# Seven block products for the last branch's gates, and blocks in the output projection

## The chip, the cores and the metric

The kernel runs on one core of a Trainium2 chip. The metric is the device time of one execution in microseconds (us), the median of several runs on the chip. Engines: PE is TensorE (matmuls), DVE is VectorE, ACT is ScalarE, POOL is GpSimd, SP issues the transfers (DMA) between DRAM and the on-chip memory. Each engine works through its own queue of instructions in order and waits there for what an instruction needs.

## The reference

Two layers of: a SwiGLU feed-forward (half weight), a token mixer, a second feed-forward, each between two RMS norms and added to a residual `x` of 512 tokens x 1024. What the change touches is the end of the mixer:

```python
def rms_norm(x, g):
    xf = x.astype(jnp.float32)
    y = xf * lax.rsqrt(jnp.mean(xf * xf, axis=-1, keepdims=True) + NORM_EPS)
    return (y * g.astype(jnp.float32)).astype(x.dtype)
...
    proj = h @ w_in                        # h = rms_norm(x, norm_pre[l, 1])
    ...
    branches = jnp.stack([sb_out, conv_out, gla_out], axis=2)         # each (512, 512)
    branch_d = jnp.einsum('bsgw,gwd->bsgd', branches, w_branch)       # to 1024
    gates = jax.nn.sigmoid(gate_logits.reshape(b, s, N_BRANCHES, D_MODEL))
    merged = jnp.sum(gates * branch_d, axis=2)
    return merged @ w_out
...
        x = x + rms_norm(m, norm_post[l, 1])
```

`gate_logits` are the last 3 x 1024 columns of `proj`. The three branches are stick-breaking attention, a depthwise convolution with layer norm, and gated linear attention.

## The kernel before

**Numbers.** Each float32 factor is split into a rounded part and a rest (`split`, `whi` and `wlo` for weights, `xh` and `xl` for the normalised input). A product is three matmuls: high by high, high by low, low by high. A weight tile arrives by DMA in `raw`, ACT casts `whi` from it, DVE subtracts to get `wlo`.

**Layout.** The mixer's input lies transposed in `xh`, `xl`: 8 k tiles of 128 channels, 512 tokens. A gate (`gate_branch`) for 128 output channels `d` is 8 k tiles x 3 matmuls with 512 tokens moving, in the bank `gate`, a sigmoid on ACT (`gs`), then the branch product: 4 k tiles x 3 matmuls in the bank `pb`, and DVE multiplies `gs<-pb,gs`. POOL adds it to `acc[d]`. `gates(g, ...)` runs over eight `d`; branch 0 (attention) fills `acc`, branch 2 (linear attention) comes next, and branch 1 (convolution) is last, because the convolution's 124 taps run on DVE beside the first two. In the loop over `gla_gates`, after the sixth gate, the convolution's norm is finished (`y<-cb`, `brl<-y`, `branch_split`).

After each gate of the last branch, `merge(d)` splits `acc[d]` into `mh`, `ml`. `out_proj` with `head=None` then multiplies them by `w_out`: 8 k tiles x 4 token tiles x 2 halves x 3 matmuls, of which the last four k tiles (`TAIL`) are done token tile by token tile, so that one tile's norm, residual and next norm (`Hand`) run beside the next tile's matmuls.

**Blocks of the feed-forward.** The feed-forward stages already use Strassen-Winograd's seven products: `block_tiles` takes two column tiles of the weights (gate and up) and two halves of the tokens as a 2 x 2 block matrix. Each product is 4 k tiles x 3 matmuls with 256 tokens moving. DVE forms sums of raw weights (`raw<-raw`); the sums of inputs are the forms `T1` to `T4` of the class `Forms`, built as the tokens arrive. `AHEAD` says how many products ahead the weights are prepared. The class `Down` does the same for the down projection, 16 of its 22 k tiles in blocks with pairs `c` (`PER` of them), and the rest plainly. Its seven products are named A12, A11, S3, S2, A22, S1, S4.

**Order.** A scheduler of the framework sets each engine's order from the program; instructions in `pinned(...)`, and all matmuls, keep the order in which they are written. The residual lies in four tiles `x_sb[i]` for the whole kernel.

Of the kernel before, what the change touches and what calls it, by code (L numbers as in the profile page):

```python
# [13 lines left out]
P = 128  # L14
D = 1024
# [26 lines left out]
def kernel(  # L42
# [19 lines left out]
    sm = ctx.enter_context(tc.tile_pool(name="sm", bufs=4))  # L62
    psp = ctx.enter_context(tc.tile_pool(name="psp", bufs=1, space=PSUM))
# [237 lines left out]
    def out_proj(w2d, nk, stat, tail, finish, upcoming, early, head=None):  # L301


        ld = lambda k: load_rows(w2d, k)
        fresh = head is None
        if fresh:
            banks = [[bank(f"o{i}{h}", "pb" if i < 3 else "pa") for h in range(2)] for i in range(NT)]
        else:
            banks, rest = head

        def mms(i, h, k, sh, sl, wh, wl):
            mm_out(banks[i][h], slice(i * P, (i + 1) * P), sh, sl, wh[:, HS[h]], wl[:, HS[h]],
                   fresh and k == 0, k == nk - 1)
# [83 lines left out]
    class Forms:  # L397
# [26 lines left out]

        def finish(self, n):
# [23 lines left out]
    def block_tiles(w0, w1, fs, forms, hid, between):  # L449
# [4 lines left out]
        silu = lambda o, i: pin(nc.scalar.activation(o, i, AF.Silu))  # L454
# [3 lines left out]
        n = 7 * len(fs)  # L458
        raw, banks, cps, ring = {}, {}, {}, {}

        def load(u):
            r = wp.tile([P, 5, 512], F32, tag="raw", name="raw", bufs=3)
            for w, q0 in ((w0, 0), (w1, 1)):
                for j in range(2):
                    nc.sync.dma_start(r[:, q0 + 2 * j].rearrange("p (k c) -> p k c", c=P),
                                      w[j * 512:(j + 1) * 512, fs[u] * P:(fs[u] + 1) * P]
                                      .rearrange("(k p) c -> p k c", p=P))
            raw[u] = r
# [46 lines left out]
        def parts(u):  # L515
            cp = cps[u]
            return [cp[:, x * 256:(x + 1) * 256] for x in range(4)], hid[fs[u]], banks[u]

        def taken(g):
# [11 lines left out]
            if j == 6:  # L531
                silu(h[:, H0], h[:, H0])
                silu(h[:, H1], A[:, H0])

        def summed(g):
# [8 lines left out]
            if j == 6:  # L544
                tt(h, cps[u][:, 512:1024], h, ALU.mult)

        for g in range(-AHEAD, n + 1):
            between(g)
            f = g + AHEAD
            if f % 7 == 0 and f < n:  # L550
                if f == 0:
                    load(0)
                if f // 7 + 1 < len(fs):
# [15 lines left out]
    class Down:  # L569
        F0, NP = 2, 8  # L570
        R1, R2 = slice(256, 512), slice(0, 256)
        PER = NP // 2
# [4 lines left out]
        MIDDLE, LAST = (0, 1), (18, 19, 20, 21)  # L577

        def __init__(self, wd, hid):
            self.wd, self.hid = wd, hid  # L580
            self.ready = {}
            self.s1 = None
# [50 lines left out]

        def sums(self, p):
# [7 lines left out]
            kept = None if j < 2 else self.kept[:, 2 * c:2 * c + 2, :].rearrange("p k c -> p (k c)")  # L642
# [4 lines left out]
            if name == "S2":  # L647
                for q, x in enumerate(self.of(p)):
                    tt(x, self.s1[c][:, q], x, ALU.add)
                tt(kept, kept, raws[0], ALU.subtract)  # L650
# [52 lines left out]
        def run(self, late):  # L703
            c0, d0, c1, d1, b0, b1 = (bank(n) for n in ("oC", "oD", "oC", "oD", "oB", "oB"))
# [3 lines left out]
            self.kept, taps = room("xh", F32), room("xl", F32)  # L708
# [8 lines left out]
            for p in range(self.end):  # L717
                j, c = self.steps[p]
                self.product(p)
                self.ahead()  # L720
# [9 lines left out]
                if j == 5:  # L730
# [13 lines left out]
            return self.out, rest  # L744
# [32 lines left out]
    def ffn(wg, wu, wd, weights, forms, arrive, finish, upcoming, early, late, begin):  # L777
# [71 lines left out]
        down = Down(wd, hid)  # L849
        block_tiles(wg, wu, fs, forms, hid, between)  # L850
# [4 lines left out]
    def mixer(l, wv, arrive, finish, upcoming, early):  # L855
# [24 lines left out]

        cw = mp.tile([P, 4, NR], F32, tag="cw", name="cw")
# [295 lines left out]
        def gate_branch(g, d, src, wb):  # L1177
# [4 lines left out]
            wh, wl = wb  # L1182
# [5 lines left out]
            return pb, sg  # L1188
# [13 lines left out]
        def gates(g, src, done):  # L1202
            for d in range(0, KC, 2):
                wb = load_branch(g, d)
                for dd in (d, d + 1):
# [7 lines left out]
                    if done is not None:  # L1213
                        done(dd)
                    yield

        sb_gates = gates(0, branch_split(sbT, "s"), None)
# [82 lines left out]
        gla_gates = gates(2, branch_split(glaT, "t"), None)  # L1300
# [24 lines left out]

        for u_ in range(KC):
            next(gla_gates)
            conv_taps(10)
            if u_ == 3:
# [18 lines left out]
        merged = []  # L1348

        def merge(d):  # L1350
            tag = "t" if d < 4 else "q"
            mh, ml = slot("mh", F32R, tag), slot("ml", F32R, tag)
            split(mh, ml, acc[d])
            merged.append((mh, ml))
# [22 lines left out]
    for idx, (l, s) in enumerate(subs):  # L1377
        norms = []

        def late():  # L1380
            norms.append(load_g(norm_post[l, s]))
            if idx + 1 < len(subs):
                norms.append(load_g(norm_pre[subs[idx + 1][0], subs[idx + 1][1]]))

        if s == 1:
            late()
# [25 lines left out]
        elif s == 1:  # L1412
            weights = mixer(l, weights, arrive, finish, upcoming, early)
# [32 lines left out]
```

## Time and profile before

| | |
|---|---|
| median of 3 runs | 2326.82 us (2326.2 to 2327.48) |
| the profiled execution | 2326.21 us, span 2324.5 us |
| PE | 2301.7 us, 99% of the span |
| DVE | 1849.0 us, 80% |
| ACT | 1220.9 us, 53% |
| POOL | 165.0 us, 7% |
| granted clock of PE | 0.999 |
| moved by DMA | 265.29 MB, mean 114 GB/s |

The span is the time between the first and the last instruction of one execution. Busy times are sums over instructions that may overlap their neighbours, so the price of one of many in a row is the distance of their starts.

### The profile page before, as it was taken

How to read it: one execution, taken by the hardware profiler on the slowest of the kernel's cores; microseconds unless marked ns; L12 is line 12 of the kernel's file. 1: busy time of each engine (PE TensorE's matmuls, PEld its weight loads, DVE VectorE, ACT ScalarE, POOL GpSimd, SP SyncE). 2: the span in 40 equal slices, each digit the busy share in tenths (PEclk: the TensorE clock that was granted, in tenths of full speed). 3: DMA queues.
4: the chain of work that ended last, by engine and by line, in shares of the span. 5: the costliest groups of instructions: out<-in, count | busy, mean ns of one | idle time of the engine just before them, and what ended most of it. 6: DMA issues, size and time to landing. Idle time of an engine off the chain costs nothing.

```text
span 2324.5 us, 35435 instructions
## 1 busy us (share of the span) xinstructions
PE 2301.7 (99%) x13688; PEld 2035.6 (88%) x13688; DVE 1849.0 (80%) x2755; ACT 1220.9 (53%) x2370; POOL 165.0 (7%) x277
## 2 busy tenths in 40 slices
PE   8999999999999999999999999999999999999998
PEld 7999888887888889998889998888878888899987
DVE  7888987859965388889888889878599644888897
ACT  5565656644323355656555666566433333566664
POOL 0000001201021100000000000022010211000000
PEclk9999999999999999999999999999999999999999
DMA  5333644131333223336433336532313332333363
GB/s 174 100 101 110 227 153 119 55 105 47 109 91 109 82 73 100 100 110 232 149 87 98 107 112 233 155 105 63 93 55 109 91 91 81 91 99 103 115 221 109
DMA packets 333019, 265.29 MB, mean 114 GB/s; under 512 B 13003, under 2 KB 285421, under 8 KB 332849
## 3 DMA queue, kind: packets, MB, share of 16 engines
q1 hardware_dynamic: 332848, 263.02, 37.3%
q8 instruction: 107, 1.75, 0.3%
q14 instruction: 64, 0.52, 0.1%
HBM read 260.88 MB, written 2.10 MB: 113 GB/s over the span
## 4 chain that ended last, share of the span: by engine, by line
PE 97%; DVE 1%; ACT 1%; issue 0%; DMA 0%; SPq 0%; DVEq 0%; POOLq 0%; ACTq 0%
PE A L66 19%; PE gate L66 11%; PE C L66 9%; PE oA L66 9%; PE pb L66 6%; PE oC L66 5%; PE B L66 5%; PE o L66 3%; PE oB L66 3%; PE pf L66 3%; PE gr L66 2%; PE pa L66 2%; PE q L66 2%; PE gv L66 2%; PE pv L66 2%; PE pgl L66 2%
## 5 line engine op out<-in xcount | busy, mean ns | idle before, releaser
L455 DVE TENSOR_TENSOR wlo<-raw,whi 128x1024 fp32r<-128x1024 f32 (+1 forms) x304 | 331.0, 1089 | 107.0 <-ACT whi L453 106.1
L453 ACT CAST whi<-raw 128x512 fp32r<-128x512 f32 x532 | 315.2, 620 | 164.7 <-DVE raw L455 164.7
L115 ACT CAST whi<-raw 128x1024 fp32r<-128x1024 f32 (+2 forms) x178 | 185.0, 1045 | 351.9 <-PE gate L66 131.4
L116 DVE TENSOR_TENSOR wlo<-raw,whi 128x1024 fp32r<-128x1024 f32 (+2 forms) x178 | 223.0, 1262 | 174.0 <-ACT whi L115 169.3
L455 DVE TENSOR_TENSOR raw<-raw 128x512 f32<-128x512 f32 x304 | 209.2, 688 | 5.7
L66 PE MATMUL A<-xh,whi 128*128 128x256 f32 x608 | 172.5, 284 | 0.0
L66 PE MATMUL A<-xh,wlo 128*128 128x256 f32 x608 | 172.0, 283 | 0.0
L66 PE MATMUL A<-xl,whi 128*128 128x256 f32 x608 | 172.0, 283 | 0.0
L1031 DVE SCALAR_TENSOR_TENSOR y<-u,cw,y 128x511 f32<-128x511 f32 (+14 forms) x240 | 166.8, 756 | 0.0
L66 PE MATMUL gate<-xh,whi 128*128 128x512 f32 x384 | 151.3, 394 | 0.0
L66 PE MATMUL gate<-xh,wlo 128*128 128x512 f32 x384 | 149.8, 390 | 1.3 <-DVE wlo L116 1.3
L66 PE MATMUL gate<-xl,whi 128*128 128x512 f32 x384 | 149.6, 390 | 0.0
L674 DVE TENSOR_TENSOR wlo<-raw,whi 128x1024 fp32r<-128x1024 f32 x104 | 127.0, 1222 | 17.5 <-ACT whi L671 17.5
L671 ACT CAST whi<-raw 128x1024 fp32r<-128x1024 f32 x104 | 109.4, 1052 | 59.3 <-issue 17.0
L268 POOL TENSOR_TENSOR rs<-ms,mhalf 128x1 f32<-128x1 f32 x44 | 25.1, 575 | 1436.9 <-DVE ms L266 1436.9
L453 ACT COPY cp<-A 128x256 f32<-128x256 f32 x228 | 84.3, 370 | 66.6 <-PE A L66 65.7
L66 PE MATMUL oA<-wlo,dh 128*128 128x512 f32 x304 | 118.6, 390 | 0.0
L66 PE MATMUL oA<-whi,dl 128*128 128x512 f32 x304 | 118.3, 389 | 0.0
L66 PE MATMUL oA<-whi,dh 128*128 128x512 f32 x304 | 118.3, 389 | 0.0
L66 PEld LDWEIGHTS A<-xl,whi 128*128 128x128 f32 x608 | 116.6, 192 | 0.2
L66 PEld LDWEIGHTS A<-xh,whi 128*128 128x128 f32 x608 | 116.5, 192 | 0.2
L66 PEld LDWEIGHTS A<-xh,wlo 128*128 128x128 f32 x608 | 116.6, 192 | 0.0
(329 smaller groups left out, 6945.6 us busy)
## 6 DMA issues: line engine op xcount, KB each, us to landing
raw<-in_ffn_w_down_dram SPq DMA_DIRECT2D x152, 512.0 KB, 4.5
raw<-in_w_in_dram SPq DMA_DIRECT2D x108, 512.0 KB, 4.7
raw<-in_ffn_w_gate_dram SPq DMA_DIRECT2D x168, 256.0 KB, 3.4
raw<-in_ffn_w_up_dram SPq DMA_DIRECT2D x168, 256.0 KB, 4.5
raw<-in_w_branch_dram SPq DMA_DIRECT2D x24, 512.0 KB, 3.6
raw<-in_w_out_dram SPq DMA_DIRECT2D x16, 512.0 KB, 4.1
g<-in_norm_pre_dram SPq DMA_DIRECT2D x6, 512.0 KB
g<-in_norm_post_dram SPq DMA_DIRECT2D x6, 512.0 KB
```

The lines of the kernel that those rows point to most:

```text
L66: tc.keep_in_program_order(nc.tensor.matmul(*a, **k))
L115: pin(nc.scalar.copy(hi, src))
L116: pin(nc.vector.tensor_tensor(lo, src, hi.bitcast(F32), op=ALU.subtract))
L268: nc.gpsimd.tensor_tensor(self.rs, ms, mhalf[:, 0:1], op=ALU.pow)
L453: copy = lambda o, i: pin(nc.scalar.copy(o, i))
L455: tt = lambda o, a, b, op: pin(nc.vector.tensor_tensor(o, a, b, op=op))
L671: pinned(nc.scalar.copy(hi, src))
L674: pinned(nc.vector.tensor_tensor(lo, src, hi.bitcast(F32), op=ALU.subtract))
L1031: nc.vector.scalar_tensor_tensor(y[:, back:], u[:, :S - back], cw[:, c, j:j + 1], y[:, back:], op0=ALU.mult, op1=ALU.add)
```

## The change

1. The last branch's gates go through `block_tiles`: four pairs of column tiles, seven products each, with `AHEAD` of 4 products (6 in the feed-forward). The branch products of a pair stay plain matmuls and stand after the pair's seven products (`branch_products`).
2. The forms `T1` to `T4` are needed in the mixer too. They are not built when the tokens arrive, but from `xh` and `xl` in `Forms.rebuild`, called after the last two gates of branch 2. `T1` and `T2` are kept in the room of the residual tiles `x0` to `x3`. The residual is stored to DRAM (`away`) at the mixer's start and loaded again (`back`) in the middle of the output projection; the two norm weights that were loaded at the mixer's start are loaded there too.
3. The output projection runs k tiles 0 to 3 through `Down` with one pair (`PER` = 1), and 4 to 7 plainly. `merge` and its splits go. The sums `down.sum` at the hand-over of tokens come in, as in the feed-forward.

The core of the diff:

```diff
+        def rebuild(self, c, room_):
+            tt = lambda o, a, b, op: nc.vector.tensor_tensor(o, a, b, op=op)
+            def whole(k0, t0):
+                r = slot("r", tag="s").rearrange("p (k t) -> p k t", k=2)
+                at = (slice(None), slice(k0 + 2 * c, k0 + 2 * c + 2), slice(t0, t0 + 256))
+                tt(r, cur["xh"][at].bitcast(F32), cur["xl"][at].bitcast(F32), ALU.add)
+                return r
+            def keep(n, r):
+                hi, lo = room_(n)
+                split(hi, lo, r)
+                self.parts.setdefault(n, [None] * 4)[2 * c:2 * c + 2] = [(hi[:, k], lo[:, k]) for k in range(2)]
+            r11, r12 = whole(0, 0), whole(0, 256)
+            tt(r12, r11, r12, ALU.subtract)
+            keep("T1", r12)
+            r22 = whole(4, 256)
+            nc.vector.scalar_tensor_tensor(r22, r12, -1.0, r22, op0=ALU.mult, op1=ALU.subtract)
+            keep("T2", r22)
+            tt(r11, r22, r11, ALU.add)
+            keep("T3", r11)
+            r21 = whole(4, 0)
+            tt(r21, r22, r21, ALU.add)
+            keep("T4", r21)
...
-        def run(self, late):
+        def run(self, late, order=("C0", "D0", "C1", "D1", "B0", "B1")):
...
                 self.product(p)
-                self.ahead()
+                if self.PER > 1:
+                    self.ahead()
...
+                    if not self.MIDDLE:
+                        sh, sl, hi, lo = self.ready[self.end]
+                        for i in range(2):
+                            mm_out(self.out[i][1], slice(i * P, (i + 1) * P), sh, sl, hi[:, HS[1]], lo[:, HS[1]], st=True)
+                if self.PER == 1:
+                    self.ahead()
...
+        away = [scr.tile([P, D], F32, tag=f"away{i}", name=f"away{i}") for i in range(NT)]
+        for i in range(NT):
+            nc.sync.dma_start(away[i], x_sb[i])
...
         for u_ in range(KC):
             next(gla_gates)
             conv_taps(10)
+            if u_ >= KC - 2:
+                mforms.rebuild(u_ - KC + 2, form_room)
...
-        for _ in gates(1, cv, merge):
-            pass
-        return out_proj(w_out[l], KC, lambda k: merged[k], TAIL, finish, upcoming, early)
+        down = Down(w_out[l], acc, 0, 2, (), (4, 5, 6, 7))
+        down.pairs()
+        PAIRS = KC // 2
...
+        def sigmoids(u, h, a, second):
+            pinned(nc.scalar.activation(h[:, H0], h[:, H0], AF.Sigmoid))
+            pinned(nc.scalar.activation(h[:, H1], a, AF.Sigmoid))
+            pinned(nc.scalar.activation(second, second, AF.Sigmoid))
...
+        def merged(u):
+            if u > 0:
+                for d in (2 * u - 2, 2 * u - 1):
+                    for n in range(2):
+                        down.sum_tokens(d, n)
+            for m, (ps, sg) in enumerate(zip(pbs[u], made[u])):
+                pinned(nc.vector.tensor_tensor(sg, ps, sg, op=ALU.mult))
+                d = 2 * u + m
+                (nc.vector if u == PAIRS - 1 else nc.gpsimd).tensor_tensor(acc[d], acc[d], sg, op=ALU.add)
+
+        def between(g):
+            u, j = divmod(g, 7)
+            if 0 <= u < PAIRS and j == 2:
+                held[0] = True
+                wbs[u] = load_branch(1, 2 * u)
+                held[0] = False
+            if u > 0 and j == 0:
+                branch_products(u - 1)
+            if u > 0 and j == 1:
+                merged(u - 1)
+            if g in (7 * PAIRS - 2, 7 * PAIRS - 1, 7 * PAIRS):
+                down.ahead()
+
+        block_tiles(source, PAIRS, mforms, target, sigmoids, between, 4)
+        merged(PAIRS - 1)
+        def back():
+            for i in range(NT):
+                if i % 2 == 0:
+                    late(i // 2)
+                x_sb[i] = resid.tile([P, D], F32, tag=f"x{i}", name=f"x{i}")
+                pinned(nc.sync.dma_start(x_sb[i], away[i]))
+
+        head = down.run(back, ("B0", "B1", "C0", "C1", "D0", "D1"))
+        return out_proj(w_out[l], KC, None, TAIL, lambda i, b: finish(i, b, down.sum), upcoming, early, head)
```

**The order on DVE at the entrance to the last branch.** Before, from the end of the convolution's norm on (`brl` are the convolution's split rests, `gs<-pb` the multiplies of the last gates of branch 2):

```order
L116 TENSOR_TENSOR brl<-y,brh 128x512
L116 TENSOR_TENSOR wlo<-raw,whi 128x1024
L116 TENSOR_TENSOR brl<-y,brh 128x512 x3
L1211 TENSOR_TENSOR gs<-pb,gs 128x512
L116 TENSOR_TENSOR wlo<-raw,whi 128x1024
L1211 TENSOR_TENSOR gs<-pb,gs 128x512
L116 TENSOR_TENSOR wlo<-raw,whi 128x1024 x2
```

After, the same place (`r` are `rebuild`'s sums, `T_...` its forms):

```order
L117 TENSOR_TENSOR brl<-y,brh 128x512 x4
L1282 TENSOR_TENSOR gs<-pb,gs 128x512
L431 TENSOR_TENSOR r<-xh,xl 128x512 x3
L431 TENSOR_TENSOR r<-r 128x512
L431 TENSOR_TENSOR r<-xh,xl 128x512
L448 SCALAR_TENSOR_TENSOR r<-r 128x512
L117 TENSOR_TENSOR T_19002<-r,T_19001 128x512
L431 TENSOR_TENSOR r<-r 128x512
L117 TENSOR_TENSOR T_19009<-r,T_19008 128x512
```

Between the two multiplies `gs<-pb` stand 13 new instructions where one `wlo` stood. The end of the second group, and the first weights of the block products (`raw<-raw` are the sums of raw weights, the first `wlo` behind them belongs to products 0 and 1):

```order
L448 SCALAR_TENSOR_TENSOR r<-r 128x512
L117 TENSOR_TENSOR T_19002<-r,T_19001 128x512
L431 TENSOR_TENSOR r<-r 128x512
L117 TENSOR_TENSOR T_19009<-r,T_19008 128x512
L431 TENSOR_TENSOR r<-r 128x512
L117 TENSOR_TENSOR T_19086<-r,T_19085 128x512
L117 TENSOR_TENSOR T_19093<-r,T_19092 128x512
L486 TENSOR_TENSOR raw<-raw 128x512 x2
L486 TENSOR_TENSOR wlo<-raw,whi 128x1024
L486 TENSOR_TENSOR raw<-raw 128x512
```

The second group has 11 instructions and stands behind the second multiply; the last branch's first weights moved behind it.

**The order of SP's transfers at the output projection.** Before (`w_out` is the projection's weight, `ffn` the next stage's):

```order
L127 DMA raw<-in_w_branch_dram 128x4x256
L127 DMA raw<-in_w_in_dram 128x8x128 x2
L127 DMA raw<-in_w_out_dram 128x1024 x8
L127 DMA raw<-in_ffn_w_gate_dram 128x2x256
L127 DMA raw<-in_ffn_w_up_dram 128x2x256
```

After (`away` is the residual in DRAM, `g` the norms' weights, the last `w_out` row the k tiles 6 and 7):

```order
L128 DMA raw<-in_w_branch_dram 128x4x256
L128 DMA raw<-in_w_out_dram 128x2x512 x8
L128 DMA raw<-in_w_out_dram 128x1024 x2
L194 DMA g<-in_norm_post_dram 128x1024
L1491 DMA x_7997<-away_4136 128x1024
L1491 DMA x_7999<-away_4137 128x1024
L194 DMA g<-in_norm_pre_dram 128x1024
L1491 DMA x_8003<-away_4138 128x1024
L1491 DMA x_8005<-away_4139 128x1024
L128 DMA raw<-in_w_out_dram 128x1024 x2
L128 DMA raw<-in_ffn_w_gate_dram 128x2x256
```

The weights of k tiles 6 and 7 moved behind six transfers.

More of the change, by code (lines that the diff above doesn't have):

```diff
@@ L447, with block_tiles @@
     AHEAD = 6
-    def block_tiles(w0, w1, fs, forms, hid, between):
+    def block_tiles(source, count, forms, target, result, between, ahead=AHEAD):
         pin = pinned
         copy = lambda o, i: pin(nc.scalar.copy(o, i))
-        silu = lambda o, i: pin(nc.scalar.activation(o, i, AF.Silu))
         tt = lambda o, a, b, op: pin(nc.vector.tensor_tensor(o, a, b, op=op))
@@ L516, in parts @@
             cp = cps[u]
-            return [cp[:, x * 256:(x + 1) * 256] for x in range(4)], hid[fs[u]], banks[u]
+            return [cp[:, x * 256:(x + 1) * 256] for x in range(4)], target(u), banks[u]
         def taken(g):
@@ L544, in summed @@
             if j == 6:
-                tt(h, cps[u][:, 512:1024], h, ALU.mult)
-        for g in range(-AHEAD, n + 1):
+                next(results[u], None)
+        for g in range(-ahead, n + 1):
             between(g)
-            f = g + AHEAD
+            f = g + ahead
             if f % 7 == 0 and f < n:
@@ L576, with __init__ @@
         AHEAD = 4
-        MIDDLE, LAST = (0, 1), (18, 19, 20, 21)
-        def __init__(self, wd, hid):
+        def __init__(self, wd, hid, f0, np, middle, last):
             self.wd, self.hid = wd, hid
+            self.F0, self.NP, self.PER = f0, np, np // 2
+            self.MIDDLE, self.LAST = middle, last
             self.ready = {}
-            self.s1 = None
+            self.s1 = self.apart = None
             self.next = 0
@@ L632, in load, with place @@
             self.raw[p] = raws
+        def place(self, n):
+            return self.kept[:, n:n + 2, :].rearrange("p k c -> p (k c)")
         def sums(self, p):
@@ L641, in sums @@
             tt = lambda o, a, b, op: pinned(nc.vector.tensor_tensor(o, a, b, op=op))
-            kept = None if j < 2 else self.kept[:, 2 * c:2 * c + 2, :].rearrange("p k c -> p (k c)")
+            kept = last = None
+            if j >= 2:
+                if self.PER == 1 and not self.apart:
+                    self.apart = [gp.tile([P, D], F32, tag="g", name="kept")]
+                elif self.PER == 1 and j == 3:
+                    self.kept = room("xh", F32)
+                    self.apart.append(self.place(0))
+                if self.PER > 1:
+                    last = kept = self.place(2 * c)
+                else:
+                    last, kept = self.apart[0], self.apart[min(j - 2, 1)]
             src = raws[0]
@@ L1378, with late @@
         norms = []
-        def late():
-            norms.append(load_g(norm_post[l, s]))
-            if idx + 1 < len(subs):
+        def late(*which):
+            if not which or 0 in which:
+                norms.append(load_g(norm_post[l, s]))
+            if idx + 1 < len(subs) and (not which or 1 in which):
                 norms.append(load_g(norm_pre[subs[idx + 1][0], subs[idx + 1][1]]))
-        if s == 1:
-            late()
         upcoming = []
@@ L1412 @@
         elif s == 1:
-            weights = mixer(l, weights, arrive, finish, upcoming, early)
+            weights = mixer(l, weights, arrive, finish, upcoming, early, late)
         else:
```

91 lines of the change are left out of this document (60 added, 31 removed).

## The prediction

> **What bounds the kernel now.** I read the page's busy shares first, then the list of waits of TensorE, then the chain in order of time, and last the timelines of single engines at the places that the change touches.
>
> ```profile
> span 2324.5 us, 35435 instructions
> PE 2301.7 (99%) x13688; PEld 2035.6 (88%) x13688; DVE 1849.0 (80%) x2755; ACT 1220.9 (53%) x2370; POOL 165.0 (7%) x277
> ...
> PE pf L66 <- ACT xh L115: 3.1, 4, 1.9
> PE pt L71 <- DVE hn L290: 2.9, 3, 1.0
> PE gate L66 <- DVE wlo L116: 1.3, 2, 0.6
> ```
>
> TensorE (PE) is busy for 2301.7 of 2324.5 us, and all its waits but those at the very start come to some 8 us. So each matmul taken out is time gained, and each wait put in is time lost, us for us. VectorE (DVE) has 20% to spare on average, but an average says nothing on one stage.
>
> The chain in order of time prices a matmul: start, length, count.
>
> ```profile
> 706.82 5.44 PE gate L66 x24
> 714.98 5.44 PE gate L66 x24
> ...
> 772.10 5.44 PE gate L66 x24
> 780.25 38.08 PE o L66 x168
> 837.02 5.49 PE pf L66 x24
> 882.27 2.88 PE A L66 x24
> 892.36 2.88 PE A L66 x24
> ```
>
> 24 gate matmuls, 512 wide, take 5.44 us: 0.2267 each; the output projection's 168 the same (38.08/168). A gate with its branch product repeats every 8.16 us. The last two rows are one feed-forward tile apart: 84 matmuls, 256 wide, in 10.09 us, 0.120 each, and no wait of PE lies between. The last branch's eight gates run from 714.98 to 780.25, the projection after them. The second layer repeats the mixer 1153 us later, so every term counts twice.
>
> **Terms that save.** (1) Gates: a pair costs 2 x 5.44 = 10.88 us now, and seven products of 12 matmuls 10.08 after: -0.80, four pairs, **-3.2** per mixer. The branch products stay as they are, 5.44 us a pair. (2) Output projection: 192 matmuls now; after, 84 for four k tiles in blocks and 96 for the other four: 12 x 0.2267 = **-2.7**. VectorE's load of a pair fits: in the feed-forward tiles it has 164.3 us of 191.5 for 19 tiles, 8.6 each, and a pair adds two multiplies and one weight split (0.69 + 0.69 + 1.22), 11.2 us beside 15.5 of PE; ScalarE's is 6.0 and some 2.
>
> ```profile
> 0.00:20.00 20.00, 10.40 (x40) 8.07 (x41) 11.80 (x23) 13.42 (x27) 2.63 (x10) 1.00 0.95 303
> 863.50:1055.00 191.50, 191.50 (x1597) 191.50 (x1596) 164.31 (x245) 113.48 (x248) 0.00 (x0) 1.00 0.36 107
> 1055.27:1142.00 86.73, 86.73 (x384) 71.78 (x384) 82.31 (x121) 55.83 (x94) 0.00 (x0) 1.00 0.64 226
> ```
>
> **The term that costs: the entrance to the last branch.** Now PE goes from the last gate of the second branch to the first of the third at 714.98 without a pause, since a gate needs only its weights. VectorE just before:
>
> ```profile
> 676.98 1.22 DVE L116 TENSOR_TENSOR wlo<-raw,whi 128x1024 fp32r<-128x1024 f32 x1 [5.58 <-ACT whi L115]
> ...
> 707.96 1.89 DVE L116 TENSOR_TENSOR brl<-y,brh 128x512 fp32r<-128x512 f32 x3
> 709.77 0.68 DVE L1211 TENSOR_TENSOR gs<-pb,gs 128x512 f32<-128x512 f32 x1
> 713.20 1.23 DVE L116 TENSOR_TENSOR wlo<-raw,whi 128x1024 fp32r<-128x1024 f32 x1 [2.75 <-ACT whi L115]
> 715.08 0.69 DVE L1211 TENSOR_TENSOR gs<-pb,gs 128x512 f32<-128x512 f32 x1 [0.66 <-PE pb L66]
> ```
>
> After, the order puts 24 instructions of `rebuild` there, in two groups of 13 and 11, each group behind a multiply `gs<-pb` that waits for PE, and the new weights' sums and `wlo` behind them all. VectorE works strictly in that order. The work ahead of it, which now ends at 709.77, loses three weight splits (some 1.14 each from start to start) and ends near 706.4. The first multiply needs the product that PE ends at 706.82; the row at 715.08 shows the lag, 0.10 behind 714.98. So it starts at 706.95. From there: multiply, 13, multiply (its product is ready at 715.08, VectorE gets there at 716), 11, two sums of raw weights: 28 instructions of 512 elements. Three such, started at 707.96, are through at 709.77: 0.603 each. 28 x 0.603 = 16.9, two of them a little longer and one wait for ScalarE's T4: 724.2. ScalarE's cast of the summed weights (0.62, row below) with two hand-overs: 725.0. `wlo` of 1024 elements (1.23, row 713.20): 726.3. The first matmul that reads it is the third of the first product, so PE stands from 714.98 for 726.3 - 715.0 - 0.2 = **+11.1** per mixer. Nothing covers it: PE's own order has nothing between. Ends of the price: 10.3 with all at 0.60 and no hand-overs, 13.5 with each at its full 0.69. Once PE runs, VectorE keeps up: products 3 and 4 need one sum, a cast and one `wlo` (0.6 + 1.2 + 1.2), PE needs 2.9 for two.
>
> ```profile
> L453 ACT CAST whi<-raw 128x512 fp32r<-128x512 f32 x532 | 315.2, 620 | 164.7 <-DVE raw L455 164.7
> 13.38 0.63 PE L66 MATMUL pf<-whi,xh 128*128 128x512 f32 x1
> ...
> 15.09 0.58 PE L66 MATMUL pf<-wlo,xh 128*128 128x512 f32 x1
> 15.50 0.40 PE L66 MATMUL pf<-whi,xl 128*128 128x512 f32 x1
> 15.74 0.39 PE L66 MATMUL pf<-whi,xh 128*128 128x512 f32 x1
> ...
> 835.73 1.29 PE L71 MATMUL pt<-ident,hn 128*128 128x128 f32 x8 [0.97 <-DVE hn L290]
> ```
>
> **(3) A slow restart.** At the start of the kernel, after standing, PE issues 512-wide matmuls 0.43 apart (13.38 to 15.09: four steps) and only from 15.50 on 0.23 apart: about 3.5 us at half rate. No row shows an idle time of 11 us in mid-run; the start is nearest, so I take **+1.6** per mixer (a bit under half of 3.5), ends 0 and 2.0. The Trainium skill, page "TensorE: Matmul & The Clock Gate", section "Part 1: The HAM clock gate", says that the array falls to half rate after an idle window of about 3.4 us and comes back after as long of steady work; by it the loss would be 1.7 each (an estimate: half of 3.4) and the time 2342.0 in place of 2341.8 below, or 2338.6 if a gap of 11 us did not count as idle. The start rows agree with it. The granted clock reads 1.00 even in the window 0 to 20, so that column does not show it.
>
> **(4) The block projection with one pair of k tiles.** Count from E, the end of the last block product. PE: branch products to E+5.4, then A12, A11, S3, S2, A22, S1 of 2.72 each, so S3 starts at E+10.9, S2 at 13.6, A22 at 16.3, S1 at 19.0, the next matmuls at 21.8. VectorE's prices:
>
> ```profile
> 1084.30 0.76 DVE L641 TENSOR_TENSOR hid<-S,hid 128x256 f32<-128x256 f32 x2
> 1084.98 1.22 DVE L641 TENSOR_TENSOR xh<-xh,raw 128x1024 f32<-128x1024 f32 x1
> 1086.11 0.76 DVE L673 TENSOR_TENSOR dl<-hid,dh 128x256 fp32r<-128x256 f32 x2
> 1086.78 1.23 DVE L674 TENSOR_TENSOR wlo<-xh,whi 128x1024 fp32r<-128x1024 f32 x1
> raw<-in_w_out_dram SPq DMA_DIRECT2D x16, 512.0 KB, 4.1
> ```
>
> 1.14 for 1024 elements, 0.67 for two of 256: a step's parts are 1.81, the sums 0.67 to 1.81 more. S3's second weights need the room of the last raw weights, which the last `wlo` of the block products frees: the third pair's branch product ends at E-10.1, and a multiply, a sum and two `wlo` (0.6 + 0.6 + 1.14 + 1.14) bring it to E-6.6. They land 4.1 later plus issue, at E-1.9. From there VectorE does S3's difference, A11's parts, the last tile's two sums, S2's sums, S3's parts (ready E+5.4), four instructions that merge the last pair (2.4), A22's sum, S2's parts (E+10.8), A22's (E+13.7), S1's (E+16.1), S4's, the fifth k tile's (E+20.1), and so on. It leads PE by 2.5 to 3 us, then 1.7, and by nothing at the last two k tiles. Their weights stand on SP's queue behind six transfers of 0.52 MB (two norms, four residual tiles), which wait for the last merge at E+7.8: 3.1 MB at the 303 GB/s of the first window take 10.4 us, and the weights land at E+22 to E+24, before ScalarE is free for them at E+24.6 (PE ends S1 at E+21.7; four copies of 512 and the cast of the sixth tile's `dh` come first). Queued behind them are only the next stage's first weights, wanted after the tokens. At the 226 GB/s of the third window they come 4 us later and PE waits. Ends 0 and +4; I take **+0.5**, nearer the first, since the queue is empty otherwise.
>
> **(5) The hand-over of tokens** gets the feed-forward's extra sums (`down.sum`).
>
> ```profile
> 1130.10 12.24 PE oA L66 x54
> 1177.43 5.46 PE pf L66 x24
> ```
>
> There 35.1 us lie between the last block matmul (1142.34) and the second `pf` group, and in the mixer 35.0 between k tile 3 (780.25 + 96 x 0.2267 = 802.0) and 837.02: hidden, nought. But six matmuls of tokens 0 and 1 now come earlier, 1.4 us, and the tail does wait for VectorE (0.97 at 835.73): **+0.5**, ends 0 and 1.4.
>
> (6) Nought: the stores of the residual at the mixer's start. SP's norm loads there wait for the same tokens (the second goes out at 367.00), and the next weights only at 374.78:
>
> ```profile
> 367.00 0.34 SPq L193 DMA_DIRECT2D g<-in_norm_pre_dram  x1
> 374.78 25.06 SPq L127 DMA_DIRECT2D raw<-in_w_in_dram  x11
> ```
>
> If that cover went, a late load would cost its 4 us once. The feed-forward stages keep their order, instruction for instruction. The dropped splits of `merged` and POOL's two adds were off the path.
>
> **Sum.** -3.2 - 2.7 + 11.1 + 1.6 + 0.5 + 0.5 = +7.8 per mixer, +15.6 in all. The profiled execution took 2326.21 (0.6 under the median of 2326.82): 2341.8, against the median 2342.4. I say **2342**. With all low ends +4.4 per mixer: 2335; with all high ends +15.0: 2356.
>
> **Rivals.** A: the gap is hidden and the kernel is faster. That is so if VectorE reaches the first `wlo` before PE ends the second branch; for it: VectorE stands idle for several us at a time some 30 us earlier (5.58 ahead of the row at 676.98), and `rebuild` reads only `xh`, `xl`. Against: in its queue the instructions stand behind a multiply tied to 706.82. Then 2326.2 - 11.8 + 2 = 2316; it decides when the gap is under 5.9 per mixer, that is when `wlo` is through by 721. B: the six transfers run at 226 GB/s or S3's weights land late, and PE waits 4 more at the projection: 2350.
>
> **Chances.** My forecast 0.71, B 0.17, A 0.09, gap and gains near each other 0.03. The range 2333 to 2352 holds the forecast and most of B. What a measurement can tell from no change is 0.2%, about 5 us: faster 0.09, same 0.03, slower 0.88.
>
> **What would show it.** Right: an idle time of PE of about 11 us before the first product `A` of each mixer, put down to VectorE's `wlo`; 256-wide matmuls about 0.21 apart for 3 us behind it; then 15.5 us per pair; less than 1 us of waits in the block projection. Wrong: the `r<-xh,xl` instructions before the multiply of 706.95, or waits on `raw` from the projection's weights.

## The result, and the profile after

The changed kernel takes 2350.41 us (median of 4 runs, 2348.38 to 2351.32), the one before 2326.99 beside it: ratio 1.010, 95% interval [1.0088, 1.0112]. It is 23.4 us slower; the forecast was 15.2 slower than its median. The profiled execution has a span of 2348.8 us against 2324.5.

The page, and TensorE's list of waits (us in total, times, longest), with two waits that the change brought:

```profile
span 2348.8 us, 36367 instructions
PE 2300.4 (98%) x13952; PEld 2042.2 (87%) x13952; DVE 1952.7 (83%) x2943; ACT 1275.9 (54%) x2510; POOL 170.7 (7%) x273
```

```profile
PE A L67 <- ACT whi L485: 17.7, 2, 8.9
PE A L67 <- DVE wlo L486: 7.0, 2, 3.5
```

Both waits at `A` are the first product of the last branch, once per mixer. The one for ScalarE's `whi` hangs on VectorE too: that cast stands in ScalarE's queue behind the casts of `T`, which wait for VectorE's sums `r`. PE's own timeline there, in the first mixer:

```profile
714.48 0.39 PE L67 MATMUL pb<-brh,wlo 128*128 128x512 f32 x1
723.73 0.58 PE L67 MATMUL A<-xh,whi 128*128 128x256 f32 x1 [8.86 <-ACT whi L485]
...
728.02 0.58 PE L67 MATMUL A<-xh,wlo 128*128 128x256 f32 x1 [3.50 <-DVE wlo L486]
728.40 0.42 PE L67 MATMUL A<-xh,whi 128*128 128x256 f32 x1
728.62 0.41 PE L67 MATMUL A<-xl,whi 128*128 128x256 f32 x1
```

The last branch product starts at 714.48 and is through at 714.71. Two matmuls slip in at 723.73; the third, the first with `wlo`, comes at 728.02. PE loses 728.02 - 714.71 - 0.24 = 13.1 us, where the sum had 11.1. Behind it the 256-wide matmuls stand 0.21 apart, not 0.12. The timelines of VectorE and GpSimd in the same stretch:

```profile
706.82 0.69 DVE L1282 TENSOR_TENSOR gs<-pb,gs 128x512 f32<-128x512 f32 x1
707.42 2.98 DVE L431 TENSOR_TENSOR r<-xh,xl 128x512 f32<-128x512 f32 x3
...
722.37 2.36 DVE L117 TENSOR_TENSOR T<-r,T 128x512 fp32r<-128x512 f32 x2
...
726.74 1.23 DVE L486 TENSOR_TENSOR wlo<-raw,whi 128x1024 fp32r<-128x1024 f32 x1 [0.68 <-ACT whi L485]
707.59 1.67 POOL L1283 TENSOR_TENSOR acc<-acc,gs 128x512 f32<-128x512 f32 x1 [7.75 <-DVE gs L1282]
717.11 7.07 POOL L1283 TENSOR_TENSOR acc<-acc,gs 128x512 f32<-128x512 f32 x1 [7.85 <-DVE gs L1282]
```

The chain is the forecast one: from the multiply at 706.82 without a pause to the `wlo` at 726.74. But three `r` sums took 2.98 us and two `T` rests 2.36, each time beside one of GpSimd's adds to `acc` (1.89 and 1.52 with the adds moved away, in the first experiment). From there the chain in order of time runs as the sum had it:

```profile
740.02 5.47 PE pb L67 x24
755.56 5.47 PE pb L67 x24
...
792.10 2.72 PE oB L67 x12
794.82 2.92 PE oA L67 x12
...
847.08 2.97 PE pf L67 x13
```

A pair comes every 15.54 us (16.32 before), and the block projection's steps stand 2.72 apart but for one of 2.92.

The rest of the loss lies outside the mixers, in the down projections of the feed-forward stages. Each engine's order of instructions there had not changed. VectorE's waits there, before and after:

```profile
DVE xh L641 <- DMA raw<-in_ffn_w_down_dram: 4.1, 8, 1.0
```

```profile
DVE xh L673 <- DMA raw<-in_ffn_w_down_dram: 8.0, 10, 1.5
```

The table has what each profile shows against the one before, worked out from starts in PE's timeline: for the two mixers from the second pair of `cb` transposes to the second `pf` group (139.17 and 139.18 before), and for three feed-forward stages: from the first mixer's second `pf` group to the start of S4 in the down projection behind it, from that S4 to the next one, and from the second mixer's second `pf` group to the S4 behind it (293.15, 340.17, 293.20 before). The runs are told below.

| kernel | median, us | ratio to before, 95% | both mixers | three feed-forward stages |
|---|---|---|---|---|
| after | 2350.41 | [1.0088, 1.0112] | +20.5 | +4.4 |
| after, again | 2349.06 (one run) | | +20.0 | +2.4 |
| before, again | 2326.30 (one run) | | 0.0 | 0.0 |
| residual away only | 2325.94 | [0.9988, 1.0006] | 0.0 | +1.1 |
| GpSimd's adds off | 2345.61 | [1.0068, 1.0095] | +16.7 | +2.9 |
| 48 idle matmuls | 2348.48 | [1.0080, 1.0107] | +19.3 | +3.2 |
| 57 idle matmuls | 2350.44 | [1.0087, 1.0115] | +20.5 | +4.1 |
| projection only, first | 2357.06 | [1.0118, 1.0145] | +30.3 | +3.1 |
| projection only, second | 2333.62 | [1.0017, 1.0038] | +5.1 | +2.2 |
| projection only, third | 2326.02 | [0.9986, 1.0004] | -1.9 | +1.0 |
| early rebuild | 2323.97 | [0.9978, 0.9996] | -6.0 (and +1.2 at `cb`) | +2.3 |
| early, late gate | 2342.95 | [1.0059, 1.0086] | +14.5 | +2.6 |
| early, weights ahead | 2318.01 | [0.9946, 0.9971] | -9.4 | +2.1 |

### The profile page after: what moved, and what is told of

Same layout as the page of the kernel before. It is cut to its first block, busy times and chain, and to the rows that moved or that the text cites. A ratio compares the mean times of both kernels' runs of the same rounds, so it can differ in the third digit from the quotient of the medians.

```text
span 2348.8 us, 36367 instructions
## 1 busy us (share of the span) xinstructions
PE 2300.4 (98%) x13952; PEld 2042.2 (87%) x13952; DVE 1952.7 (83%) x2943; ACT 1275.9 (54%) x2510; POOL 170.7 (7%) x273
## 4 chain that ended last, share of the span: by engine, by line
PE 91%; DVE 5%; ACT 1%; issue 1%; DMA 1%; SPq 0%; POOL 0%; DVEq 0%; POOLq 0%; ACTq 0%
PE A L67 21%; PE C L67 10%; PE oA L67 9%; PE gate L67 7%; PE oC L67 5%; PE B L67 5%; PE pb L67 5%; PE oB L67 3%; PE pf L67 3%; PE gr L67 2%; PE pa L67 2%; PE q L67 2%; PE gv L67 2%; PE pv L67 2%; PE pgl L67 2%; PE k L67 2%
## 5 line engine op out<-in xcount | busy, mean ns | idle before, releaser
L486 DVE TENSOR_TENSOR wlo<-raw,whi 128x1024 fp32r<-128x1024 f32 (+1 forms) x336 | 366.0, 1089 | 124.9 <-ACT whi L485 124.1
L485 ACT CAST whi<-raw 128x512 fp32r<-128x512 f32 x588 | 349.1, 620 | 187.4 <-DVE raw L486 182.3
L116 ACT CAST whi<-raw 128x1024 fp32r<-128x1024 f32 (+2 forms) x146 | 151.2, 1043 | 241.2 <-PE gate L67 73.6
L117 DVE TENSOR_TENSOR wlo<-raw,whi 128x1024 fp32r<-128x1024 f32 (+2 forms) x146 | 174.8, 1207 | 98.0 <-ACT whi L116 94.5
L486 DVE TENSOR_TENSOR raw<-raw 128x512 f32<-128x512 f32 x336 | 232.3, 691 | 6.1
L717 DVE TENSOR_TENSOR wlo<-raw,whi 128x1024 fp32r<-128x1024 f32 x122 | 148.9, 1220 | 17.7 <-ACT whi L714 17.7
L67 PE MATMUL oA<-wlo,dh 128*128 128x512 f32 x352 | 138.6, 394 | 0.2 <-DVE wlo L717 0.2
L67 PE MATMUL gate<-xh,whi 128*128 128x512 f32 x256 | 101.5, 396 | 0.0
L67 PE MATMUL gate<-xh,wlo 128*128 128x512 f32 x256 | 100.0, 391 | 1.3 <-DVE wlo L117 1.3
L67 PE MATMUL gate<-xl,whi 128*128 128x512 f32 x256 | 99.8, 390 | 0.0
```

The costliest lines, as they stand in the source:

```text
L67: tc.keep_in_program_order(nc.tensor.matmul(*a, **k))
L116: pin(nc.scalar.copy(hi, src))
L117: pin(nc.vector.tensor_tensor(lo, src, hi.bitcast(F32), op=ALU.subtract))
L485: copy = lambda o, i: pin(nc.scalar.copy(o, i))
L486: tt = lambda o, a, b, op: pin(nc.vector.tensor_tensor(o, a, b, op=op))
L717: pinned(nc.vector.tensor_tensor(lo, src, hi.bitcast(F32), op=ALU.subtract))
```

## The experiments

**GpSimd's adds off.** The theory: the gap is 2 us longer than the sum because GpSimd's adds stretch VectorE's chain.

```diff
+                        if g == 2 and dd >= KC - 2:
+                            kept_back.append((dd, sg))
+                            yield
+                            continue
                         nc.gpsimd.tensor_tensor(acc[dd], acc[dd], sg, op=ALU.add)
...
+            if g == 3:
+                for d, sg in kept_back:
+                    pinned(nc.vector.tensor_tensor(acc[d], acc[d], sg, op=ALU.add))
```

> The changed kernel, with GpSimd's adds to acc for the last two gates of the second branch done by VectorE later, at product 3 of the first pair, where it has time. Theory: VectorE's chain of 28 instructions is stretched by GpSimd working in the same memory beside it (the r sums at 707.42 took 2.98 us in place of 1.8, the T rests at 722.37 took 2.36 in place of 1.3). Then the idle time of PE before the first product falls from 13.1 us to about 10.9 per mixer, near the 11.1 of the sum, and the kernel takes 4.4 us less: about 2346. Rival: those long rows have another cause, and the GpSimd add only sits there; then the idle time stays at 13.1 and the time at 2350.4.

2345.61, 4.8 less than the changed kernel. The timelines of VectorE and PE in this run: the three sums and the two rests are short again.

```profile
708.80 1.89 DVE L431 TENSOR_TENSOR r<-xh,xl 128x512 f32<-128x512 f32 x3
...
722.63 1.52 DVE L117 TENSOR_TENSOR T<-r,T 128x512 fp32r<-128x512 f32 x2
```

```profile
715.85 0.39 PE L67 MATMUL pb<-brh,wlo 128*128 128x512 f32 x1
...
727.44 0.58 PE L67 MATMUL A<-xh,wlo 128*128 128x256 f32 x1 [2.65 <-DVE wlo L486]
```

PE now loses 727.44 - 716.08 - 0.24 = 11.1 us there, the sum's own figure. In the profiles the two mixers gained 3.8 us and the feed-forward stages 1.5; the second is less than the difference between the changed kernel's own two profiles (4.4 and 2.4). The theory holds; the two adds cost VectorE 1.1 and 0.8 us per mixer.

**Idle matmuls in the gap.** The theory: the matmuls 0.21 apart are a slow restart of PE after standing.

```diff
+            if g == 0:
+                warm = bank("warm", "pa")
+                for _ in range(48):
+                    mm(warm, cv[0][0][:, 0:P], cv[0][0], start=True, stop=True)
```

> The changed kernel, with 48 matmuls of 512 columns into a spare bank between the last branch product of the second branch and the first block product; nothing reads them, and they fill about 10.9 of the 13.1 us for which PE stands there. Theory of the cold restart: the 256-wide matmuls that stood 0.213 apart for 4 us stand 0.12 apart from the first on, and each mixer gains 2.0 us: 2346.4 in all. Rival: they are paced by what VectorE or ScalarE deliver, not by PE's own rate; then nothing changes, 2350.4. If the filling itself gets in the way (the products start later than now), the time grows.

2348.48: 1.9 less, not 4.0. PE stood 2.07 us for `wlo` behind the filling, and in the first mixer a stretch at half rate came all the same (in the second fence two windows, with the granted clock in the third column from the right); in the second mixer, with the same wait, none.

```profile
728.00 0.39 PE L67 MATMUL A<-xh,wlo 128*128 128x256 f32 x1 [2.07 <-DVE wlo L486]
```

```profile
726.00:731.00 5.00, 3.00 (x15) 3.00 (x16) 3.08 (x4) 2.91 (x6) 0.00 (x0) 0.74 0.02 3
1886.00:1899.00 13.00, 10.93 (x67) 9.62 (x66) 10.86 (x14) 7.32 (x15) 4.00 (x1) 1.00 0.01 1
```

> The changed kernel with 57 idle matmuls in the gap in place of 48, 12.9 us of the 13.3. With 48, PE still stood 2.07 us before the third matmul of the first product; in the first mixer a stretch of 3.4 us at half rate followed all the same, and in the second none, and 1.9 us were gained in place of 4.0. Theory: that rest is what started the stretch; with PE standing under 0.5 us, both mixers restart at full rate, 4.0 us less than the changed kernel: about 2346.4. Rival: the rate falls for another reason, at the change from one kind of matmul to another; then 2348.5 again.

With 57, 2350.44: no gain at all, though the theory of the clock holds: the granted clock stays at 1.00 behind the gap. Windows and VectorE's timeline of this run, and the same `kept` in the changed kernel:

```profile
727.00:732.00 5.00, 4.98 (x34) 4.37 (x32) 3.23 (x4) 2.98 (x7) 0.00 (x0) 1.00 0.01 3
```

```profile
787.11 1.22 DVE L673 TENSOR_TENSOR kept<-raw 128x1024 f32<-128x1024 f32 x1 [3.02 <-DMA raw<-in_w_out_dram]
```

```profile
786.08 1.22 DVE L673 TENSOR_TENSOR kept<-raw 128x1024 f32<-128x1024 f32 x1 [1.50 <-DMA raw<-in_w_out_dram]
```

From the last plain branch product's first matmul to the first pair's branch products it is 26.64 us (712.72 to 739.36) against 27.86 (711.99 to 739.85), and in the second mixer 26.92 against 28.16: the clock is worth 1.2 us per mixer. The other 0.8 of the slow first tile (10.6 us for 82 matmuls that need 9.8) is VectorE and ScalarE, which prepare the weights just in time. The 1.2 were lost again later: the projection's weights landed 1.0 us later though the mixer ran 0.5 earlier, VectorE waited 3.02 in place of 1.50 for them, and the first two block steps took 3.62 and 3.50 in place of 2.72 and 2.92 (starts 791.45, 795.07, 798.57), 1.5 us. The second mixer lost 1.1 in the same place. They were not asked for later: the two weights whose room the last `wlo` of the block products frees were issued at 781.85 and 782.26, 0.5 us earlier than in the changed kernel (782.35 and 782.76). So the transfers themselves took longer; why is not settled.

**The projection alone.** Gates plain, no `rebuild`, the residual stays:

```diff
-        block_tiles(source, PAIRS, mforms, target, sigmoids, between, 4)
-        merged(PAIRS - 1)
+        for dd, _ in enumerate(gates(1, cv)):
+            if dd == 4:
+                for d in (2, 3):
+                    for n in range(2):
+                        down.sum_tokens(d, n)
+            if dd >= 5:
+                down.ahead()
```

> Only the output projection in blocks: the last branch's gates are plain as before the change, no rebuild, and the residual stays where it was. Theory: no idle time at the entrance; per mixer 12 matmuls fewer in the projection (-2.72), of which 0.7 is lost at the hand-over of tokens and 0.2 to a wait: -1.8, so -3.7 in all, 2323.3 against 2327.0 before, if the feed-forward stages keep their time; 2327.6 if their 4.3 us of waits for down weights come with the projection. Rival: with plain gates beside it VectorE can't prepare the pair's steps in time, PE waits 2 or more per mixer at the projection, and the kernel is no faster than before.

2357.06: the worst of all. PE's timeline shows it stand at the last two gates, and then go 0.43 per matmul for 4 us:

```profile
770.20 0.80 PE L67 MATMUL gate<-xh,wlo 128*128 128x512 f32 x1 [3.81 <-DVE wlo L117]
770.80 0.63 PE L67 MATMUL gate<-xh,whi 128*128 128x512 f32 x1
771.22 0.63 PE L67 MATMUL gate<-xl,whi 128*128 128x512 f32 x1
...
785.90 0.80 PE L67 MATMUL gate<-xh,wlo 128*128 128x512 f32 x1 [4.46 <-DVE wlo L117]
```

The pinned first steps of the projection (`dl`, `wlo`, `kept`) stood in VectorE's queue ahead of the gates' own `wlo`. That is the order of this experiment, not the projection. Second try, the three `down.ahead()` behind the last gate's matmuls:

```diff
                     pb, sg = gate_branch(g, dd, src, wb[dd - d])
+                    if g == 1 and dd == KC - 1:
+                        for _ in range(3):
+                            down.ahead()
```

> Only the output projection in blocks, with the weights of the last two gates now prepared ahead of the projection's first steps (in the first such run the gates' wlo stood behind them on VectorE, and PE waited 3.8 and 4.5 us per mixer, each followed by a stretch at half rate). Theory: that order was all that went wrong, and the projection itself gives what the trace of the changed kernel shows, -1.8 per mixer: 2323.3 with the feed-forward stages as before, up to 2326.5 with the 3 us more that they took in all the changed kernels' traces. Rival: the pair's steps don't fit beside plain gates on VectorE; PE waits 2 or more at the projection, and the time is 2327 to 2332.

2333.62. Now the last gate's sigmoid held up ScalarE, and VectorE behind it:

```profile
777.36 0.60 ACT L1246 ACTIVATE gs<-gate 128x512 f32<-128x512 f32 x1 [7.56 <-PE gate L67]
777.86 0.70 ACT L713 CAST dh<-acc 128x256 fp32r<-128x256 f32 x2
778.28 0.76 DVE L716 TENSOR_TENSOR dl<-acc,dh 128x256 fp32r<-128x256 f32 x2 [4.94 <-ACT dh L713]
```

Third try: the last gate's weights first, then two steps, then its matmuls and its (pinned) sigmoid.

```diff
+                    if g == 1 and dd == KC - 1:
+                        ready_w[g, dd] = load_cols(W, C_GATE + g * D + dd * P)
+                        for _ in range(2):
+                            down.ahead()
                     pb, sg = gate_branch(g, dd, src, wb[dd - d])
```

> Only the output projection in blocks, with plain gates. In the run before it (2333.62) the last gate's sigmoid, which waits for that gate's matmuls, stood ahead of the first casts of the projection on ScalarE; VectorE stood idle 4.94 us for them, started the projection's weights at E-1.5 in place of E-8, and the block steps took 40.0 us in place of 35.6. Now the first two steps' casts stand ahead of that sigmoid, behind the last gate's weights. Theory: the steps take 36 us; per mixer -1.8 against the kernel before, and 2 to 3 us more in the feed-forward stages, as in every changed kernel: 2325 to 2326, 2323.3 if those stages keep their time. Rival: the steps need VectorE's lead of a block pair and are late with plain gates in any order; then 2330 or more.

2326.02 against 2327.16, no measurable difference (interval [0.9986, 1.0004]). The theory holds in kind: per mixer -1.0, not -1.8, since the later steps still wait a little (36.5 us from `oB` to the next stage's first transposes, 35.6 in the early run below). So of the whole change the projection alone is worth about 1 us per mixer.

**The rebuild moved.** The theory: VectorE's order at the entrance is the whole cause of the gap. `rebuild` goes to the third and fifth gate of the second branch, and the last multiply behind the first weights:

```diff
-            if u_ >= KC - 2:
-                mforms.rebuild(u_ - KC + 2, form_room)
+            if u_ in (2, 4):
+                mforms.rebuild(u_ // 2 - 1, form_room)
...
+            if g == -2:
+                pb, sg = kept_back.pop()
+                pinned(nc.vector.tensor_tensor(sg, pb, sg, op=ALU.mult))
...
```

> The whole change, with rebuild at the third and fifth gate of the second branch, where VectorE stands idle for 4 to 6 us at a time (the rests of T3 and T4 for the second half lie in the room that the linear attention's transposed output leaves), and the multiply of the branch's last gate after the first weights of the block products. Theory: the order of VectorE is the whole cause of the idle time, so it goes with it, and the slow restart too: per mixer -13.1 - 2.0 against the changed kernel, which leaves -4.9 against the one before; in all 2317 if the feed-forward stages go back to their time, 2321.5 if their waits of 4.3 stay. Rival: VectorE or ScalarE fall behind in the second branch instead, PE waits there for wlo or for the multiplies' bank, and the kernel stays above 2327.

2323.97, faster than both kernels, 2.5 above the theory's 2321.5. The gap is gone, and so is the half rate. What is left (the first three products take 1.8 us each, not 1.44, and the transposes `cb` wait 0.6): the last gate's sigmoid stands ahead of the first casts on ScalarE, and VectorE waits for them:

```profile
713.12 0.60 ACT L1250 ACTIVATE gs<-gate 128x512 f32<-128x512 f32 x1 [6.14 <-PE gate L67]
713.62 1.13 ACT L485 CAST whi<-raw 128x512 fp32r<-128x512 f32 x2
714.78 1.22 DVE L486 TENSOR_TENSOR wlo<-raw,whi 128x1024 fp32r<-128x1024 f32 x1 [5.99 <-ACT whi L485]
```

The next run wrote that gate behind the preparation of products 0 and 1 (`next(gla_gates)` in `between(-2)`):

> As the run with the early rebuild, but the last gate of the second branch is now written behind the preparation of products 0 and 1, so that ScalarE casts their weights ahead of that gate's sigmoid, and the second half of rebuild stands behind the norm's statistics of tokens 2 and 3. In the early run the first three products took 1.76 us each in place of 1.44, since ScalarE's cast stood behind the sigmoid of 713.12 (VectorE idle 5.99 ahead of the wlo at 714.78), and the transposes cb waited 0.6 for yn. Theory: both waits go, about 2 us per mixer: some 4 us less than the early run's 2324.0, so 2320. Rival: VectorE has too much to do in these 20 us, and the wait only moves to another product; then 2323 to 2325.

2342.95, a miss of 23 us: the gate's own weights now stood behind the products' weights, and PE waited for them.

```profile
PE gate L67 <- DVE wlo L117: 10.1, 4, 4.4
...
PE gate L67 <- ACT whi L116: 7.0, 2, 3.5
```

So that gate's weights are loaded first:

```diff
+            if u_ == KC - 2:
+                ready_w[2, KC - 1] = load_cols(W, C_GATE + 2 * D + (KC - 1) * P)
...
+            if g == -2:
+                next(gla_gates)
+            if g == 0:
+                pb, sg = kept_back.pop()
+                pinned(nc.vector.tensor_tensor(sg, pb, sg, op=ALU.mult))
+                nc.gpsimd.tensor_tensor(acc[KC - 1], acc[KC - 1], sg, op=ALU.add)
```

Here `next` writes that gate's matmuls and its sigmoid, which is now pinned.

> The early rebuild, mended once more. In the run before it (2342.95) the weights of the last gate of the second branch stood behind those of products 0 and 1 on ScalarE and VectorE, and PE waited 3.5 and 4.4 us per mixer for them. Now that gate's weights are prepared first, its matmuls and its sigmoid stand behind the casts of products 0 and 1, and its multiply behind the rests of products 2 and 3. Theory: all waits at the entrance go; per mixer 1.5 us of late products and 0.6 at the transposes less than in the first early run, so 4 in all: 2324.0 - 4 = 2320. Rival: moving work ahead in full queues only moves the wait (as it did in the run before); then it stays at 2323 or above.

2318.01, ratio 0.9959 [0.9946, 0.9971]: 9.1 us faster than the kernel before and 32.4 faster than the change as made. PE's timeline passes the entrance without a pause, at full rate, and from there to the hand-over of tokens its list of waits has only 0.2 us, at `oA` in one mixer:

```profile
714.44 0.39 PE L67 MATMUL pb<-brh,wlo 128*128 128x512 f32 x1
714.67 0.28 PE L67 MATMUL A<-xh,whi 128*128 128x256 f32 x1
714.78 0.28 PE L67 MATMUL A<-xl,whi 128*128 128x256 f32 x1
```

**The feed-forward stages.** Is their 4.4 us the change's, and is it the residual's traffic? The kernel before, with the residual stored at the mixer's start and loaded ahead of `out_proj`:

```diff
+        for i in range(NT):
+            nc.sync.dma_start(away[i], x_sb[i])
...
+        for i in range(NT):
+            x_sb[i] = resid.tile([P, D], F32, tag=f"x{i}", name=f"x{i}")
+            pinned(nc.sync.dma_start(x_sb[i], away[i]))
```

> The kernel before, with nothing of the change but the residual's way out: stored to DRAM at each mixer's start and loaded again before the output projection, 2 MB each way. Term 6 says nought for it. If the 1 to 4 us that the changed kernels lose in the feed-forward stages come from this traffic, or from where it puts things in DRAM, the three stages exceed their 293.15, 340.17 and 293.20 us by as much here, and the time is 2328 to 2331; if not, 2327.0 and the same stages within 0.3.

> The kernel before once more, for its profile alone. Its three feed-forward stages after the first mixer took 293.15, 340.17 and 293.20 us between like points. If the time there varies from run to run, this run is off by a microsecond or more in one of them; if the 4.3 us that the changed kernel lost there belong to the change, this run is within 0.3 of these numbers in each.

> The changed kernel once more, for its profile alone. The three stages took 295.31, 341.44 and 294.13 us in its first profile, 4.4 more than before. If that belongs to the change, it repeats within 0.5 in sum; if it is the luck of one run, the sum of the excess falls anywhere from 0 to 5.

The residual's way out costs nothing that can be measured: 2325.94 against 2326.43, its mixers the same to 0.01 us. The kernel before repeats its three stages to 0.1 us; the changed kernel's excess there was 4.4 in one profile and 2.4 in the other. The eleven profiles with the block projection have 1.0 to 4.4 in sum, 2.8 in the mean, the one with the residual away alone 1.1. VectorE's waits for `raw<-in_ffn_w_down_dram` tell the same: 3.5 to 4.8 us in the three profiles of the old program, 4.7 to 8.0 in the others. So in these profiles the weights land later in the changed programs, by an amount that varies, and the two ranges touch; what makes them late stays open.

## Why the prediction was right, and where its sum was off

The direction, the place and the mechanism were as forecast, and 2350.4 lies in the range; the forecast 2342 is 8 us short. By its own steps, per mixer:

- **Gates, -3.2.** Right: 15.54 us per pair against 16.32, four times -0.78 is -3.1.
- **Projection, -2.7.** Right in count. Alone it brought -1.0, the hand-over and late steps taking the rest.
- **The gap, +11.1.** Right cause, shown by the early run; mis-sized: 13.1. The step that failed is "28 x 0.603", which took VectorE's instructions as undisturbed. The adds `acc` that GpSimd starts behind each multiply `gs<-pb` were costed as "off the path"; they are off PE's path and lengthen VectorE's chain, and without them the gap is the forecast 11.1. The range's upper end (13.5) covered it by another reason.
- **Slow restart, +1.6.** 2.0 measured for the first tile, of which the runs with idle matmuls give 1.2 to the clock and 0.8 to weights prepared just in time, which the sum had as nought ("VectorE keeps up"). The clock column does show such a stretch (0.74 in a row of the run with 48 idle matmuls); the 1.00 read in the window 0 to 20 said nothing of the start, because the clock record of that profile has no entry before 15.48 us.
- **Block projection, +0.5.** 0.2. Rival B's price of 4 did not come, and its six transfers were not waited for; that the measured time is the 2350 that it gave is luck. Its other half, S3's weights landing late, is real and near: VectorE waited 1.50 us for `raw` (the row at 786.08), which the prediction had named as a sign against itself. PE lost 0.2 us here, and 1.5 in the run with 57 idle matmuls.
- **Hand-over, +0.5.** 0.7: from the first token's last matmul to the second `pf` group it takes 29.5 us as before (817.61 to 847.08, 807.45 to 837.02), so six matmuls saved there bring nothing.
- **Residual, nought.** Right, shown by itself.
- **Not in the sum:** the feed-forward stages, taken as unchanged because their order is. +4.4 in the first profile, 2.4 in the second.

Mixers +10.2 and +10.3 in place of 7.8 twice, and 4.4 outside, make the 24.3 us between the two spans (0.5 less at the kernel's end). Rival A, the gap hidden, was a matter of the order alone: with `rebuild` in VectorE's idle time and the first weights ahead of the last gate's sigmoid the kernel takes 2318, near the 2316 that A gave.

## What to carry to other kernels

Ask of each block of work that a change adds not only whether its engine has time on average, but behind which waiting instruction it stands in that engine's queue, and who needs it first; the same instructions cost 13 us at one place and nothing 20 to 40 us earlier. When work is pulled ahead, look at every queue that it passes (ScalarE's sigmoids, the next gate's own weights), since three of these runs ended 7 to 30 us above the kernel before for that. An engine called "off the path" can still slow the one on it: GpSimd's two adds lengthened VectorE's chain by 1.9 us per mixer.

## What the runs showed of the hardware

- A GpSimd add of 128x512 on the on-chip memory, started beside VectorE's stream of two-input sums, lengthened that stream by 1.1 and 0.8 us (2.98 against 1.89, 2.36 against 1.52). VectorE left no pause at either place, yet the first add took 1.67 us and the second 7.07. The Trainium skill, page "SBUF — State Buffer", section "SBUF: two separate sides", says that the two engines share a pair of ports as an exclusive lock, where such a VectorE instruction and a GpSimd instruction shut each other out; the rows agree that each engine held the other up, but no run here shows that a lock is the reason.
- The clock record of these traces shows half rate in stretches of 3.41, 6.83, 10.24 and 13.65 us, one to four times 3.41. Stands of 13.1 us, of 3.8 and 4.5 us, and in one case of 2.07 us started one; another of 2.07 us did not. Counted from its first entry, the record changes only at whole multiples of 3.41 us. With each profile cut into steps of that length, every step at full rate in which PE stood for 2.07 us or more in sum was followed by half rate, in all 14 profiles, and none was in which it stood for 1.87 us or less. That tells the two stands of 2.07 us apart: the one lay within a single step (724.98 to 728.39), the other was divided between two, 0.56 and 1.51 us. The Trainium skill, page "TensorE: Matmul & The Clock Gate", section "Part 1: The HAM clock gate", has the window of 3.4 us and that it runs freely; the runs agree in that, but the stretch after a stand of 2.07 us came without the full idle window of 3.4 us that it asks for.
- A saving on PE can be lost to a transfer that takes longer for no reason that the program shows: with 57 idle matmuls the weights were issued 0.5 us earlier and landed 1.0 us later.
